# A wait ahead of the sampled tokens' memory-key products and other pauses in a hybrid decoder step

## The chip, the cores and the metric

The kernel runs on one core of one Trainium2 chip, in one launch. The metric is the device time of that launch in microseconds (us). Three runs of the kernel before took 2145.94, 2152.03 and 2154.46 us, so the median is 2152.03 us.

## What is computed

One step of a one-layer hybrid decoder, for a prompt of 1024 tokens and for 8 sampled tokens of other sequences. A norm and one wide projection feed four head groups (differential attention A, RWKV-7 B, Mamba-2 C, cross-attention X into 256 memory tokens); each group's output is gated, the four are concatenated, and a second projection and a last norm follow. What the change touches is X for the samples and the output of C. Cut to these, and with what they read:

```python
h = rmsnorm(x, lp['norm_g'])
p = h @ lp['w_in']
dq, dk, dvv, dg, rs, rg, mz, mxbc, mdt, xq, xg = split_in(p)
...
ym, ssm_new = ssd_scan(xh * dt[..., None], A * dt, bh, chh, ssm_state.astype(f32), chunk)
ym = ym + lp['d_skip'][:, None] * xh
out_m = rmsnorm(ym.reshape(b, t, BRANCH) * jax.nn.silu(mz.astype(f32)), lp['gnorm_g'])
...
qx = xq.reshape(b, t, H_X, D_X)
s = jnp.einsum('bqhd,bmhd->bhqm', qx, mem_k.astype(qx.dtype), preferred_element_type=f32) * (D_X ** -0.5)
pm = jax.nn.softmax(s, axis=-1)
ox = jnp.einsum('bhqm,bmhd->bqhd', pm, mem_v.astype(f32))
out_x = ox.reshape(b, t, BRANCH) * jax.nn.silu(xg.astype(f32))

mixed = jnp.concatenate([out_a, out_b, out_m, out_x], axis=-1).astype(xdtype)
x = x + mixed @ lp['w_out']
```

## The kernel before

**The stream of projections.** The 1024 prompt tokens and 8 sample tokens are three groups of 344 columns. A block of 128 output columns of `w_in` or `w_out` is 16 tiles of the contraction times three groups, and each product is three matmuls, since every float is split into a high and a low part (`hh`, `hl` of the activations, `whi`, `wlo` of the weights). A block is cut into four pieces of four contraction tiles; a piece's weights come by one DMA of 256 KB on SyncE's queue (`raw`, L525) and are split by ScalarE (`whi`, L541) and VectorE (`wlo`, L542). These matmuls (`acc`, L565) are the bulk of TensorE's work; a narrow block for the Mamba step sizes is L583. A finished group is evacuated by ScalarE and VectorE (`evs` L678 to L687 for the RWKV columns, `evg` and `evo` L751 to L754 for the gates).

**The lanes.** The four head groups are written as Python generators, the lanes. A driver hands out instructions while the program is built. It keeps a clock of its own, `K.now`, that only TensorE instructions advance; a lane that says `yield 2.5` is asked again when that clock is 2.5 further, and in between the driver issues matmuls of the projection stream. `yield from K.wait("x")` holds a lane until another lane has said `K.mark("x")`. So a pause sets how many `acc` matmuls stand on TensorE between two steps of a lane. Under this sits the framework's scheduler, which gives each engine its final order; a VectorE instruction needs not stand there in the order in which the lanes issued it.

**Stages.** Lanes run in stages, each with its own memory pools: first A for the prompt; then `lane_x` (cross-attention of the prompt, 4 heads of 4 query blocks) beside `lane_sa` (A and then X for the samples); then RWKV in three lanes, `products`, `elements` and `norm`, beside `lane_b` (the samples' RWKV); then the step sizes, and Mamba's eight chunks in `mixer_m` beside `samples_m`; then the output projection. A stage begins when every lane of the one before has ended.

**Around the change.** `samples_x` runs 22 turns over 16 tiles of the memory keys (`sxkp`, 128 x 512, loaded by GpSimd's queue, 8 buffers). From the seventh turn on a tile is multiplied by its query, spread over the partitions (`sxqb`, loaded on SyncE's queue), and summed by head into `sxsc`; these are two VectorE instructions each, L1766 and L1767. Then come transposes of the scores (`p_sxs`), a softmax, transposes of the weights (`p_sxw`), and 11 turns over the memory values (`sxvp`, products `p_sxo`, columns picked by `p_vc` into `sxo`). On the same VectorE the prompt's `lane_x` takes maxima (`xm` L1715), and divides by the row sums (`xe` L1721) ahead of TensorE's transposes `p_xt`.

After that stage the RWKV stage loads its constants (`cst` L842, `up` L845), a strip of decay inputs (`lw` L864, a tanh on ScalarE, L865) and the first rows (`rkv` L870), and its first matmuls are `p_lora` from `lw` and `up`, then transposes `p_kn` of `kk` and `p_kb` of `rx`.

In `mixer_m`, a chunk's output `my` is multiplied by its gate (L1341, from the transposes `p_mg`), squared and summed (L1344), scaled (L1347) and transposed (`p_my`). A pause of 3.6 stands ahead of `p_my`.

Of the kernel before, what the change touches and what calls it, by code (L numbers as in the profile page):

```python
# [1255 lines left out]
def mixer_m(K, P, dt):  # L1256
# [15 lines left out]
    for c in range(8):  # L1272
        t0 = c * 128
        r8 = nxt
        x = P.tile([128, 4, 128], F32, name="mxx", tag="mxx")
# [69 lines left out]
        nc.vector.tensor_scalar(ss[:, 0:1], ss[:, 0:1], 0.25 / 512, RMS_EPS, op0=ALU.mult, op1=ALU.add)  # L1345
        K.powm(ss[:, 1:2], ss[:, 0:1], 1)
        nc.vector.tensor_scalar(flat(y), flat(y), ss[:, 1:2], 0.5, op0=ALU.mult, op1=ALU.mult)  # L1347
        yield 3.6
        p = K.ps("p_my", 1)
        for b in range(4):  # L1350
            K.tp(p[:, b * 128:b * 128 + 128], flat(y[:, 2 * b:2 * b + 2, :]), K.id)
# [221 lines left out]
def value_columns(K, P, po, o, half, ring, **slot):  # L1573

    nc = K.nc
    e = P.tile([128, 512], F32, name="vce", **slot)
    nc.scalar.copy(e, po)
    yield 1.0
    p = K.ps("p_vc", ring)
    for b in range(4):  # L1580
        K.tp(p[:, b * 128:b * 128 + 128], e[:, b * 128:b * 128 + 128], K.id)
    nc.vector.tensor_copy(out=o.rearrange("p (h b) -> p b h", h=4)[:, 4 * half:4 * half + 4, :],
                          in_=p.rearrange("p (b h r) -> p b h r", b=4, h=4)[:, :, :, 0])
# [156 lines left out]
def samples_x(K, P):  # L1740
    nc, I = K.nc, K.I
    x = P.tile([128, 8, 4], F32, name="sxx", tag="sxx")
# [11 lines left out]
    for i in range(16 + 6):  # L1754
        if i < 16:
            if i % 2 == 0:
                qb = P.tile([128, 512], F32, name="sxqb", tag="sxqb", bufs=4)
                nc.sync.dma_start(out=qb, in_=K.svX[i // 2 * 4:i // 2 * 4 + 4].rearrange(
                    "(o h) c -> o (h c)", o=1).to_broadcast([128, 512]))
            kp = P.tile([128, 512], F32, name="sxkp", tag="sxkp", bufs=8)  # L1760
            nc.gpsimd.dma_start(out=kp, in_=I["cache_mem_k"][i // 2, i % 2 * 128:i % 2 * 128 + 128])
            ahead.append((kp, qb))
        if i >= 6:
            b, a = (i - 6) // 2, (i - 6) % 2
            kp, q = ahead.pop(0)
            nc.vector.tensor_tensor(kp, kp, q, op=ALU.mult)  # L1766
            nc.vector.tensor_reduce(sc[:, a, b * 4:b * 4 + 4], kp.rearrange("p (h c) -> p h c", h=4), axis=AX.X, op=ALU.add)  # L1767
        yield 2.5 if i >= 6 else 1.2
    yield 8.92
    p = K.ps("p_sxs", 0)  # L1770
    for a in range(2):
# [16 lines left out]
    for b in range(8 + 3):  # L1788
        if b < 8:
            vp = [P.tile([128, 512], F32, name="sxvp", tag="sxkp", bufs=8) for a in range(2)]  # L1790
            for a in range(2):
                nc.gpsimd.dma_start(out=vp[a], in_=I["cache_mem_v"][b, a * 128:a * 128 + 128])
            ahead.append(vp)
        yield 4.0 if b > 2 else 1.5
        if b < 3:
            continue
        vp, b = ahead.pop(0), b - 3
        if b % 4 == 0:
            po = K.ps("p_sxo", 0)
        for a in range(2):  # L1800
            for h in range(4):
                q = slice(32 * h, 32 * h + 32)
                K.mm(po[q, (b % 4) * 128:(b % 4) * 128 + 128], lhsT=w[:, a, b * 4 + h:b * 4 + h + 1].to_broadcast([128, 32]),
                     rhs=vp[a][:, h * 128:h * 128 + 128], start=a == 0, stop=a == 1)
        if b % 4 == 3:
            yield from value_columns(K, P, po, o, b // 4, 0, tag="vce")
# [234 lines left out]
def lane_m(K):  # L2041
    yield from K.wait("mz3", 0.00)
    with K.tc.tile_pool(name="mmp", bufs=1, side="right") as P:
        yield from mixer_m(K, P, K.dt)
    K.mark("m")


def lane_sa(K):

    pool = lambda n: K.tc.tile_pool(name=n, bufs=1, side="right")  # L2050
    with pool("sap") as P:
        yield from samples_a(K, P)
    K.mark("sa")
    with pool("sxp") as P:
        yield from samples_x(K, P)
    K.mark("sx")
# [84 lines left out]
```

## Time and profile before

| | |
|---|---|
| median of three runs | 2152.03 us |
| the profiled execution, its own time | 2149.52 us |
| its span from the first to the last instruction | 2147.8 us |
| TensorE, matmuls | 2086.2 us busy, 97% of the span |
| TensorE, weight loads | 1979.4 us busy, 92% |
| VectorE | 1145.8 us, 53% |
| ScalarE | 839.1 us, 39% |
| mean granted TensorE clock | 0.993 of full speed |

TensorE's matmuls and weight loads overlap each other. The span less the matmuls' busy time, 61.6 us, is what TensorE spent without a matmul. The other engines' shares say little by themselves: they count only where TensorE waits for one of them.

### The profile page before, as it was taken

The numbers are of one execution on the slowest core, as the hardware profiler recorded it, in microseconds if no ns is written. First come the engines' busy times: TensorE is split into PE (matmuls) and PEld (weight loads), VectorE is DVE, ScalarE is ACT, GpSimd is POOL, SyncE is SP. The second block draws the span as 40 slices with busy tenths as digits, with TensorE's granted clock in tenths as the row PEclk, the third lists the DMA queues.
The fourth block names the chain that finished last, engine by engine and source line by source line (L and its number), as shares of the span: only waits on it lengthen the run. The fifth ranks groups of instructions, "written<-read, shape, count | busy, mean of one in ns | idle before, by whom it ended". The sixth has DMA issues, their size and how long they took to land.

```text
span 2147.8 us, 41628 instructions
## 1 busy us (share of the span) xinstructions
PE 2086.2 (97%) x16260; PEld 1979.4 (92%) x16260; DVE 1145.8 (53%) x2795; ACT 839.1 (39%) x2231; POOL 203.4 (9%) x286
## 2 busy tenths in 40 slices
PE   8999999999999999999999999999999999999997
PEld 6799999999999989988888888889999999999997
DVE  5724353533643352158877776755966354333554
ACT  6724354443113322145455444432122144333544
POOL 2100000000622210011110010001100000000000
PEclk9999999999999999999999999999999999999998
DMA  7643425242844462332222222226644583222881
GB/s 256 194 131 92 133 76 151 70 128 59 244 144 140 143 217 67 105 74 74 71 69 60 53 61 65 58 67 156 184 137 133 169 253 102 73 73 70 245 247 53
DMA packets 336925, 263.12 MB, mean 123 GB/s; under 512 B 62204, under 2 KB 310986, under 8 KB 336032
## 3 DMA queue, kind: packets, MB, share of 16 engines
q1 hardware_dynamic: 323744, 218.64, 36.3%
q0 software_dynamic: 12320, 40.28, 6.2%
q8 instruction: 128, 2.10, 0.4%
q10 hardware_dynamic: 664, 1.54, 0.2%
q14 instruction: 69, 0.57, 0.1%
HBM read 205.65 MB, written 54.80 MB: 121 GB/s over the span
## 4 chain that ended last, share of the span: by engine, by line
PE 79%; DVE 7%; DMA 5%; issue 4%; ACT 4%; POOL 2%; SPq 0%; ACTq 0%; DVEq 0%; POOLq 0%
PE acc L565 62%; PE p_s L1507 2%; PE p_t L186 2%; PE p_o L186 2%; DMA raw<-in_w_in 1%; DVE wlo L542 1%; DVE evc L716 1%; PE p_wt L190 1%; PE p_out L190 1%; PE acc L583 1%; PE p_xo L186 1%; POOL gst L216 1%; PE p_xs L186 1%; PE p_yd L186 1%; DMA xt<-in_x_prompt 1%
## 5 line engine op out<-in xcount | busy, mean ns | idle before, releaser
L565 PE MATMUL acc<-hh,whi 128*128 128x344 f32 x3312 | 1074.4, 324 | 8.9 <-DVE evg L752 2.9
L565 PE MATMUL acc<-hl,whi 128*128 128x344 f32 x3312 | 1077.2, 325 | 0.0
L565 PE MATMUL acc<-hh,wlo 128*128 128x344 f32 x3312 | 1075.6, 325 | 1.2 <-DVE wlo L542 0.8
L565 PEld LDWEIGHTS acc<-hh,whi 128*128 128x128 f32 x3312 | 624.5, 189 | 15.9 <-DVE evg L752 4.1
L565 PEld LDWEIGHTS acc<-hl,whi 128*128 128x128 f32 x3312 | 625.7, 189 | 5.1 <-issue 0.6
L565 PEld LDWEIGHTS acc<-hh,wlo 128*128 128x128 f32 x3312 | 622.9, 188 | 8.0 <-DVE wlo L542 3.1
L542 DVE TENSOR_TENSOR wlo<-raw,whi 128x512 fp32r<-128x512 f32 x300 | 207.1, 690 | 463.8 <-ACT whi L541 462.4
L541 ACT CAST whi<-raw 128x512 fp32r<-128x512 f32 x300 | 185.5, 618 | 443.9 <-PE acc L565 407.5
L186 PEld LDWEIGHTS p_t<-rt,lt 64*64 64x64 f32 x1280 | 44.6, 134 | 33.6 <-issue 13.3
L1832 ACT ACTIVATE p_out<-xo 128x128 f32<-128x128 f32 (+1 forms) x144 | 39.9, 277 | 77.4 <-DVE xo L1831 73.1
L186 PE MATMUL p_t<-rt,lt 64*64 64x64 f32 (+1 forms) x1280 | 54.3, 223 | 15.8 <-DVE lt L973 7.3
L1510 DVE CUSTOM_DVE_ANT_0 ae<-p_s,al 128x512 f32<-128x512 f32 (+3 forms) x96 | 49.6, 554 | 34.9 <-PE p_s L1507 34.9
L1517 ACT ACTIVATE ae<-ae,am 128x128 f32<-128x128 f32 (+7 forms) x64 | 49.2, 772 | 10.9 <-DVE am L1514 10.8
L1831 DVE TENSOR_TENSOR xo<-xo,p_out 128x128 f32<-128x128 f32 (+1 forms) x144 | 39.4, 280 | 26.0 <-PE p_out L190 25.7
L979 ACT COPY rt<-p_t 128x256 f32<-128x256 f32 x64 | 22.0, 344 | 77.3 <-DVE xc L971 72.7
L542 DVE TENSOR_TENSOR wlo<-oraw,whi 128x512 fp32r<-128x512 f32 x48 | 33.2, 692 | 31.7 <-ACT whi L541 31.4
L216 POOL TENSOR_TENSOR osr<-osr,mhalf 128x1 f32<-128x1 f32 (+1 forms) x9 | 6.4, 725 | 461.4 <-DMA xo<-in_x_prompt 337.6
L216 POOL TENSOR_TENSOR ass<-ass,mhalf 128x8 f32<-128x8 f32 x4 | 6.6, 1642 | 423.3 <-DVE ass L1558 423.3
L1507 PE MATMUL p_s<-akm,aqt 128*128 128x512 f32 (+3 forms) x192 | 45.1, 360 | 0.0
L1618 POOL DMA_INDIRECT sakp<-in_cache_diff_k,sapt x32 | 42.0, 1313 | 31.2 <-DMA xmk<-smk 18.1
L541 ACT CAST whi<-oraw 128x512 fp32r<-128x512 f32 x48 | 29.7, 618 | 32.5 <-PE acc L565 31.1
L1834 DVE TENSOR_TENSOR xo<-xo,fgc 128x128 f32<-128x128 f32 (+1 forms) x96 | 27.0, 288 | 28.7 <-ACT p_out L1832 27.6
(467 smaller groups left out, 2587.0 us busy)
## 6 DMA issues: line engine op xcount, KB each, us to landing
raw<-in_w_in SPq DMA_DIRECT2D x220, 256.0 KB
raw<-in_w_out SPq DMA_DIRECT2D x80, 256.0 KB
oraw<-in_w_out SPq DMA_DIRECT2D x12, 1024.0 KB
evm<-sm SPq DMA_DIRECT2D x48, 172.0 KB
sB<-evs SPq DMA_DIRECT2D x39, 172.0 KB
sA<-evp SPq DMA_DIRECT2D x36, 172.0 KB
evo<-so SPq DMA_DIRECT2D x36, 172.0 KB
sm<-evo SPq DMA_DIRECT2D x36, 172.0 KB
```

Source lines behind the costliest of these rows:

```text
L186: self.nc.tensor.matmul(out, lhsT=lhsT, rhs=rhs, start=start, stop=stop, **k)
L190: self.nc.tensor.transpose(out, in_, ident)
L216: self.nc.gpsimd.tensor_tensor(out, x, self.mhalf[:P, :n], op=ALU.pow)
L541: nc.scalar.copy(hi, raw)
L542: nc.vector.tensor_tensor(lo, raw, hi.bitcast(F32), op=ALU.subtract)
L565: nc.tensor.matmul(acc[g][:, :G], lhsT=x[:, k, :], rhs=y, start=kp == ko[0] and k == 0 and x is hi and y is a, stop=kp == ko[-1] and k == ...
L1507: nc.tensor.matmul(p[:, :k1 - k0], lhsT=qt[:, a, c], rhs=km[:, c, k0:k1], start=a == 0, stop=a == 1)
L1510: nc.vector.tensor_tensor_reduce(e[:, c, k0:k1], p[:, :k1 - k0], al[:, x0:x0 + k1 - k0], 1.0, -3e38, ALU.add, ALU.max, m[:, c, pc:pc + 1])
L1517: nc.scalar.activation(e[:, c, :nk], e[:, c, :nk], AF.Exp, bias=m[:, c, 0:1], accum_out=z[:, c:c + 1])
L1618: nc.gpsimd.indirect_dma_start(out=dst, out_offset=None, in_=I[src].rearrange("a p c -> (a p) c"), in_offset=bass.IndirectOffsetOnAxis(ap= ...
L1831: nc.vector.tensor_tensor(xt, xt, q[:n, k * 128:k * 128 + 128], op=ALU.add)
L1832: nc.scalar.activation(q[:n, k * 128:k * 128 + 128], xt, AF.Square, accum_out=self.ss[:n, 3 * g + k, cb:cb + 1])
```

## The change

Three pauses and one wait are changed. `samples_x` waits for the end of the prompt's cross-attention before it issues the first product of a memory key; its turns from there on pause 1.8 where they paused 2.5; the turns over the memory values pause 3.0 where they paused 4.0. In the first of Mamba's eight chunks the pause ahead of `p_my` is 5.0 where it was 3.6. No instruction is added or taken away.

```diff
@@ -1345,7 +1345,7 @@
-        yield 3.6
+        yield 3.6 if c else 5.0
         p = K.ps("p_my", 1)
@@ -1760,12 +1760,14 @@
             ahead.append((kp, qb))
+        if i == 6:
+            yield from K.wait("x")
         if i >= 6:
             b, a = (i - 6) // 2, (i - 6) % 2
             kp, q = ahead.pop(0)
             nc.vector.tensor_tensor(kp, kp, q, op=ALU.mult)
             nc.vector.tensor_reduce(sc[:, a, b * 4:b * 4 + 4], kp.rearrange("p (h c) -> p h c", h=4), axis=AX.X, op=ALU.add)
-        yield 2.5 if i >= 6 else 1.2
+        yield 1.8 if i >= 6 else 1.2
     yield 8.92
@@ -1791,7 +1793,7 @@
-        yield 4.0 if b > 2 else 1.5
+        yield 3.0 if b > 2 else 1.5
```

How the built program's order changes is shown at three places. The lines of `samples_x` stand two further down in the changed file, so L1766 and L1767 there are L1768 and L1769.

First VectorE, where the products of the memory keys (`sxkp`, `sxsc`) begin, among the prompt's maxima and divisions (`xm`, `xe`) and a split of weights (`wlo`). Before:

```order
L1766 TENSOR_TENSOR sxkp<-sxkp,sxqb 128x512 x2
L1767 TENSOR_REDUCE sxsc<-sxkp 128x4
L542 TENSOR_TENSOR wlo<-raw,whi 128x512
L1767 TENSOR_REDUCE sxsc<-sxkp 128x4
L1715 TENSOR_REDUCE xm<-p_xs 128x2
L1766 TENSOR_TENSOR sxkp<-sxkp,sxqb 128x512
L1716 TENSOR_SCALAR xm<-xm 128x2
L1766 TENSOR_TENSOR sxkp<-sxkp,sxqb 128x512
L1767 TENSOR_REDUCE sxsc<-sxkp 128x4
L1720 RECIPROCAL xm<-xm 128x2
L1767 TENSOR_REDUCE sxsc<-sxkp 128x4
L1721 TENSOR_TENSOR xe<-xe,xm 128x512
```

With the change:

```order
L1768 TENSOR_TENSOR sxkp<-sxkp,sxqb 128x512 x2
L1769 TENSOR_REDUCE sxsc<-sxkp 128x4
L542 TENSOR_TENSOR wlo<-raw,whi 128x512
L1769 TENSOR_REDUCE sxsc<-sxkp 128x4
L1715 TENSOR_REDUCE xm<-p_xs 128x2
L1768 TENSOR_TENSOR sxkp<-sxkp,sxqb 128x512
L1716 TENSOR_SCALAR xm<-xm 128x2
L1768 TENSOR_TENSOR sxkp<-sxkp,sxqb 128x512
L1769 TENSOR_REDUCE sxsc<-sxkp 128x4
L1720 RECIPROCAL xm<-xm 128x2
L1769 TENSOR_REDUCE sxsc<-sxkp 128x4
L1721 TENSOR_TENSOR xe<-xe,xm 128x512
```

Nothing moved here: row for row it is the same order, and it stays the same on VectorE until the maximum over the scores `p_sxs`. On TensorE the first row that differs is the pair of transposes `p_sxs` itself, which stand behind 184 more `acc` matmuls than before (3960 against 3776, counted from the program's start).

Second SyncE's queue, where the last of the samples' cross-attention (`so<-sxo`) is followed by the first loads of the RWKV stage. Before:

```order
L525 DMA raw<-in_w_in 128x4x8 x2
L1807 DMA so<-sxo 128x4x8
L842 DMA cst_9313<-in_cst 128x992
L525 DMA raw<-in_w_in 128x4x8
L845 DMA up<-in_up 128x512
L864 DMA lw<-sB 128x256
L870 DMA rkv<-sB 128x4x64
L687 DMA sB<-evs 128x344
L870 DMA rkv<-sB 128x4x64
```

With the change:

```order
L525 DMA raw<-in_w_in 128x4x128 x2
L1809 DMA so<-sxo 128x4x8
L842 DMA cst_9479<-in_cst 128x992
L525 DMA raw<-in_w_in 128x4x128
L845 DMA up<-in_up 128x512
L864 DMA lw<-sB 128x256
L870 DMA rkv<-sB 128x4x64
L525 DMA raw<-in_w_in 128x4x128
L870 DMA rkv<-sB 128x4x64 x2
```

The queue's own order is nearly the same, but the place moved against TensorE: between the last `p_vc` and the first `p_lora` there stand 48 `acc` matmuls, where 120 stood; from the first `p_lora` to the first `p_z` there are 148, where 172 stood. From the program's start the first `p_lora` stands behind 48 more `acc` matmuls, and the end of the RWKV lanes behind 24 more.

Third VectorE in the first Mamba chunk, where `my` is gated (L1341) and scaled (L1347); L1282 is the scan over the next chunk's decays, `evg` and `evo` are the evacuation of a gate block. Before:

```order
L1335 TENSOR_TENSOR St<-St,p_st 128x512
L1282 SCALAR_TENSOR_TENSOR r_17170<-r_17170,lt 128x1024
L1341 TENSOR_TENSOR my<-my,p_mg 128x512
L542 TENSOR_TENSOR wlo<-raw,whi 128x512
L1345 TENSOR_SCALAR myss<-myss 128x1
L1347 TENSOR_SCALAR my<-my,myss 128x512
L752 SCALAR_TENSOR_TENSOR evg<-evg,acc_17021 128x344
```

With the change:

```order
L1335 TENSOR_TENSOR St<-St,p_st 128x512
L1282 SCALAR_TENSOR_TENSOR r_17194<-r_17194,lt 128x1024
L752 SCALAR_TENSOR_TENSOR evg<-evg,acc_17021 128x344
L753 SCALAR_TENSOR_TENSOR evo<-evg,evo 128x344
L1341 TENSOR_TENSOR my<-my,p_mg 128x512
L752 SCALAR_TENSOR_TENSOR evg<-evg,acc_17022 128x344
L753 SCALAR_TENSOR_TENSOR evo<-evg,evo 128x344
L1345 TENSOR_SCALAR myss<-myss 128x1
L1347 TENSOR_SCALAR my<-my,myss 128x512
```

Four evacuating instructions now stand ahead of the scaled `my`, where one split of weights stood. On TensorE 36 `acc` matmuls stand between the transposes `p_mg` and `p_my` of this chunk, where 28 stood.

## Rows read from the trace of the kernel before

**Rows 1.** The page's first part: span, busy time of each engine.

```profile
span 2147.8 us, 41628 instructions
PE 2086.2 (97%) x16260; PEld 1979.4 (92%) x16260; DVE 1145.8 (53%) x2795; ACT 839.1 (39%) x2231; POOL 203.4 (9%) x286
```

**Rows 2.** Busy time by stretch: start:end, length, engines, clock, DMA share, GB/s.

```profile
906.00:935.00 29.00, 29.00 (x197) 24.38 (x195) 7.61 (x24) 12.12 (x33) 2.72 (x6) 1.00 0.37 95
935.00:1445.00 510.00, 492.00 (x5804) 440.83 (x5803) 380.78 (x1009) 235.35 (x708) 55.04 (x102) 1.00 0.25 64
1490.00:1500.00 10.00, 7.38 (x50) 7.06 (x49) 5.22 (x8) 3.03 (x7) 0.57 (x1) 1.00 0.39 116
1500.00:1690.00 190.00, 189.04 (x1251) 185.43 (x1251) 128.09 (x195) 38.95 (x76) 10.04 (x16) 1.00 0.51 144
771.30:778.00 6.70, 5.42 (x18) 5.09 (x19) 5.91 (x10) 1.09 (x3) 2.25 (x5) 0.51 0.88 264
...
1054.60:1058.00 3.40, 3.40 (x16) 3.34 (x15) 3.40 (x10) 3.04 (x10) 1.42 (x4) 0.52 0.66 188
```

**Rows 3.** Waits of TensorE, 680 to 800: in total, times, longest (us).

```profile
PE p_xt L190 <- DVE xe L1721: 4.1, 2, 3.6
```

**Rows 4.** VectorE in order of time, 738 to 792: start, us, instruction, idle before.

```profile
760.05 1.30 DVE L1766 TENSOR_TENSOR sxkp<-sxkp,sxqb 128x512 f32<-128x512 f32 x2 [8.07 <-DMA sxqb<-svX]
```

**Rows 5.** TensorE in order of time, 765 to 782.

```profile
768.47 0.32 PE L565 MATMUL acc<-hl,whi 128*128 128x344 f32 x1
768.63 0.32 PE L565 MATMUL acc<-hh,wlo 128*128 128x344 f32 x1
772.58 1.09 PE L190 MATMUL p_xt<-cst,xe 128*128 128x128 f32 x4 [3.63 <-DVE xe L1721]
```

**Rows 6.** DMA issues: line engine, count, KB each, us to landing.

```profile
sxvp<-in_cache_mem_v POOLq DMA_DIRECT2D x16, 256.0 KB, 3.5
```

**Rows 7.** The start of the RWKV stage, 900 to 945, TensorE in order of time.

```profile
905.62 0.60 PE L190 MATMUL p_vc<-cst,vce 128*128 128x128 f32 x4
...
926.44 1.57 PE L186 MATMUL p_lora<-lw,up 64*128 64x128 f32 x16
...
931.11 0.38 PE L190 MATMUL p_kn<-cst,kk 128*128 128x128 f32 x2
```

**Rows 8.** The same stretch on SyncE's queue, then ScalarE, then VectorE.

```profile
906.47 0.37 SPq L1807 DMA_DIRECT2D so<-sxo  x1
...
910.82 0.42 SPq L864 DMA_DIRECT2D lw<-sB  x1
...
914.20 0.42 ACT L865 ACTIVATE lw<-lw 64x256 f32<-64x256 f32 x1 [0.45 <-DMA lw<-sB]
...
916.46 0.42 DVE L786 TENSOR_TENSOR kk<-rkv,pt 128x256 f32<-128x256 f32 x1
...
934.93 0.29 DVE L800 COPY rx<-rn 128x256 f32<-128x256 f32 x1 [0.95 <-POOL rn L216]
```

**Rows 9.** TensorE right behind: the transposes that need `rx`.

```profile
935.28 0.44 PE L190 MATMUL p_kb<-cst,rx 128*128 128x128 f32 x2
```

**Rows 10.** Waits of TensorE, 906 to 1445: the first of ten rows.

```profile
PE p_t L186 <- DVE lt L973: 7.3, 9, 2.3
```

**Rows 11.** VectorE in the first Mamba chunk, in order of time, 1490 to 1505.

```profile
1493.69 2.29 DVE L1282 TENSOR_TENSOR_SCAN r<-r,lt 128x1024 f32<-128x1024 f32 x1 [2.90 <-DMA r<-sda]
1495.90 0.66 DVE L1341 TENSOR_TENSOR my<-my,p_mg 128x512 f32<-128x512 f32 x1
...
1499.22 0.49 DVE L1347 TENSOR_SCALAR my<-my,myss 128x512 f32<-128x512 f32 x1 [0.69 <-POOL myss L216]
1499.62 0.51 DVE L752 SCALAR_TENSOR_TENSOR evg<-evg,acc 128x344 f32<-128x344 f32 x1
```

**Rows 12.** TensorE there: the transposes that need `my`.

```profile
1499.85 0.63 PE L190 MATMUL p_my<-cst,my 128*128 128x128 f32 x4 [2.62 <-DVE my L1347]
```

**Rows 13.** ScalarE there: the squares of `my`, in order of time.

```profile
1497.63 0.63 ACT L1344 ACTIVATE mysq<-my 128x512 f32<-128x512 f32 x1
```

## The prediction, made before the changed kernel ran

> **What bounds the kernel now.** I read the page's first part, then the table of stretches, then TensorE's waits in the stretches that the change touches, and last the order of time around each wait. The first part shows TensorE with a matmul in flight for 2086.2 of 2147.8 us [rows 1]: the time of this kernel is TensorE's work plus 61.6 us of holes. The change adds and removes no instruction, so it can only fill or open holes, or change the clock in which matmuls run. The reader is to look for three things in the table of stretches [rows 2]: how much of each stretch is without a matmul, whether the granted clock is 1.00, and which stretch comes behind a step that moves. In the stage of the cross-attentions the holes are two, both for `xe` and 4.1 us together [rows 3]; the first 29 us of the RWKV stage have none; the remaining 510 us of that stage have 18.0; around the first chunk's `p_my` 2.6 of 10 us are lost; the rest of the Mamba stage loses 1.0 in 190 [rows 2].
>
> Where the larger hole for `xe` comes from is told by the order of time. VectorE came to the first two products of memory keys and stood 8.07 us for `sxqb` [rows 4]; the maxima and divisions of the prompt's attention stood behind them, and TensorE, whose matmuls start 0.16 us apart at full clock, stood 3.63 us for `xe` at 772.58 [rows 5]. Then the clock fell: from 771.3 to 778.0 the granted clock was 0.51, that is 1.2 in place of 2.4 GHz [rows 2].
>
> **The change, part by part.**
>
> *The wait for the prompt's attention, and the pause of 1.8.* The words of the change would take that hole away: 4.1 us of waits, and the slow clock behind them. Of the slow stretch, 772.58 to 778.0 had matmuls, 5.4 us at half speed, so 2.7 us lost; 6.8 us in all. The page "TensorE: Matmul & The Clock Gate" of the Trainium skill (Terms) puts the penalty at the throttled time multiplied by one minus the granted share; its estimate here is 6.7 x 0.5 = 3.4 us and 7.5 in all, as it also counts the 1.3 us in which TensorE had nothing to run. But the built order, shown above, says that nothing of this happens. On VectorE the products stand exactly where they stood, the wait for `sxqb` is still ahead of the same `xe`, and no row of TensorE differs before `p_sxs`. A pause of a lane spaces TensorE's steps; the scheduler below puts a VectorE product where VectorE is free, and the two instructions in question have no TensorE step ahead of them in their lane. I take 0 for this part; the ends are 0 and a gain of 6.8.
>
> *The tail of the samples' cross-attention, later by 184 matmuls.* `p_sxs` and all behind it move down TensorE's stream by some 29 us. What hides it is the stream itself: between two turns of memory values there are 24 `acc` matmuls in place of 32, 3.8 us in place of 5.1. A tile of values is loaded four turns ahead, at least 15 us, and lands in 3.5 [rows 6]. Nobody but the gates of X waits for the result, and they come hundreds of us later. 0 us; if the cover were gone, a late tile would stop TensorE for what is left of those 3.5 us.
>
> *The start of the RWKV stage, which is now close behind.* This is where something new can wait. Before, 120 `acc` matmuls lay between the last `p_vc` and `p_lora`; now 48. So 72 x 0.16 = 11.5 us of cover go. Before, the tanh of `lw` ended at 914.62 and `p_lora` began at 926.44 [rows 7, 8]: 11.8 us of slack, of which 0.3 is left. The chain ahead of it is the same: `so<-sxo`, then the load of constants, a weight load, `up`, `lw`; 8.4 us from the end of `p_vc` (906.22) to the end of the tanh [rows 7, 8], on a queue on which a weight load that waits for VectorE holds up those behind it. `kk` ended at 916.88 and `p_kn` began at 931.11 [rows 7, 8]: 14.2 us, and 76 matmuls fewer (the 72, and 16 in place of 20 behind `p_lora`) take 12.2, so 2.0 are left; its second load of rows now stands behind a weight load. `rx` ended at 935.22 and `p_kb` began at 935.28 [rows 8, 9], no slack at all, and there are 14 matmuls in place of 24 between `p_kn` and `p_kb`: up to 1.6 us of wait, less what ScalarE and VectorE save because the evacuation of the narrow block (`evd`) is now over by then. Up to `p_z` the first unit has 24 matmuls fewer, so it can lose 3.8 us at most as long as its loads are in time. Ends 0 and 3.8; I take 1.0, nearer the low end, because only the last of the three steps has no slack.
>
> *The other units of the RWKV stage.* All of it stands 24 to 48 matmuls later against the lanes, so its meetings with the evacuation of projection blocks are dealt anew. Its 18.0 us of holes [rows 2] are mostly `p_t` waiting for `lt`, 7.3 us in 9 times [rows 10]. In the order I counted, over the 64 rounds, the VectorE instructions that stand between a round's transpose and its mask `lt`: 36 before, 40 now. In proportion, 7.3 x 4 / 36 = +0.8 us. The page "Perfetto Trace Analysis" (Optimization Strategy) says that the same gap repeating on the engine that should be saturated can mean too few buffers; if so the order would not matter, and this term would be 0 and the sum 0.8 lower. The rows name VectorE's `lt`, not a buffer, as what ended these waits, so I keep +0.8. For the ends I take half of the 18.0 us either way, +9 and -9.
>
> *The pause of 5.0 in the first Mamba chunk.* `p_my` waited 2.62 us for `my` [rows 12]. Eight matmuls more ahead of it are 1.3 us of cover. Against that, two evacuating instructions, 0.51 us each [rows 11], now stand ahead of the gated `my`. But ScalarE began its squares at 1497.63 [rows 13], 1.07 us after the gated `my` was there at 1496.56 [rows 11], being busy with other work; so nearly all of that 1.0 us is free. The second pair falls beside the squares. I take 0.3 us of delay and a gain of 1.0; ends 0 and 1.3. A part of the wait stays in any case. No clock to win: it was 1.00 through that hole [rows 2]. In the other seven chunks the lanes of prompt and samples stand 1.4 apart from where they stood; with 1.0 us of holes in 190 [rows 2] I take 0, ends -1 and +1.
>
> **The sum:** 0 + 0 + 1.0 + 0.8 - 1.0 + 0 = +0.8 us. Against the profiled execution's own 2149.52 that is 2150.3. That execution lies 2.5 us under the median of the three runs, 2152.03; for the median I forecast 2152.8. About 0.5%, 10.8 us, is what a measurement of this kernel can tell from no change.
>
> **The rivals.**
>
> 1. *A late load stops the RWKV stage, and the change is slower.* The place is the first `p_lora`, the price is that of the hole for `xe`. For it: of 11.8 us of slack 0.3 is left, and the chain of five DMAs stands on a queue that weight loads can hold up. Against it: a delay of 1 or 2 us costs just that, and the hole of 2.62 us left the clock at 1.00; behind the one of 3.63 it fell, and once in the RWKV stage, for 3.4 us behind the longest hole there, of 2.3 [rows 2, 5, 10, 12]. So it decides when the tanh of `lw` ends over 10.5 us behind `p_vc`, 2 us and more later than the 8.4 of before. Then 3.6 + 2.7 for clock, and 3.8 in `p_kn` to `p_z` in place of 1.0: +9.1 more, 2161.9, and with a bad deal of the units beyond 2163. By the clock page's estimate of 3.4 in place of 2.7 it would be 2162.6. Chance 0.10.
> 2. *The units of the RWKV stage fall well.* Half of the holes or more are gone: 2152.8 - 9.8 = 2143, more in the best case. For it: nothing but chance decides which evacuation stands ahead of which `lt`. Against it: the count of 40 against 36. Chance 0.09.
> 3. *The products do move.* Then 6.8 us go: 2146.0. For it only the words of the change; against it the order, row for row. Chance 0.03.
>
> The forecast, little change because the named move does not take place, has 0.78.
>
> **How the numbers follow.** The forecast's own spread, from the ends of the terms, is 2144 to 2161. The range reaches down into the second rival and up to the first: 2143 to 2162. Faster by over 0.5% needs under 2141.3: the better part of the second rival, 0.06. Slower by over 0.5% needs over 2162.8: half of the first rival and a bad deal without it, 0.09. Within 0.5%: 0.85.
>
> **What the new profile would show.** Right: the hole for `xe` of about 3.6 us and the clock at half behind it, at the same place and unchanged; `p_sxs` some 29 us later; `p_lora` less than 10 us behind the last `p_vc`, with holes of 2 us at most there and at `p_kn` and `p_kb`; the hole at the first `p_my` smaller by about 1 us, not gone. Wrong: no wait for `xe` between 765 and 780, which would make the third rival true; a hole over 3 us at `p_lora` with a granted clock of 0.5 behind it, the first; holes of the RWKV stage far from 18 us, the second or its opposite.

## The result and the profile after

Four runs of the changed kernel took 2171.93 to 2173.36 us, median 2172.12; the kernel before, on the same chip, 2150.03 (four runs). The ratio is 1.0096, with a 95% interval of 1.0071 to 1.0121: slower by 22 us. The forecast was 2152.8 and the range ended at 2162, so it was wrong, and on the side to which it gave 0.09.

The page's first part of the kernel after, to be read against [rows 1]:

```profile
span 2170.4 us, 41611 instructions
PE 2098.4 (97%) x16260; PEld 1987.4 (92%) x16260; DVE 1144.9 (53%) x2795; ACT 841.6 (39%) x2231; POOL 202.0 (9%) x286
```

The same 16260 matmuls, 22.6 us more of span. Of these 10.4 are TensorE without a matmul (72.0 us where it was 61.6), and 12.2 are matmuls that took longer. The table of stretches of the kernel after (columns as in [rows 2]) shows a part of both:

```profile
774.60:778.00 3.40, 2.30 (x9) 2.33 (x10) 3.40 (x7) 0.62 (x2) 1.07 (x2) 0.57 0.95 283
935.00:1455.70 520.70, 502.77 (x5843) 447.69 (x5843) 383.01 (x1017) 241.18 (x721) 56.85 (x103) 1.00 0.25 64
1502.83:1509.60 6.77, 6.77 (x28) 6.47 (x29) 2.71 (x5) 0.00 (x0) 0.00 (x0) 0.55 0.39 128
...
1596.80:1600.20 3.40, 3.37 (x16) 3.40 (x17) 0.69 (x1) 0.00 (x0) 0.00 (x0) 0.63 0.50 142
1753.30:1756.70 3.40, 3.38 (x16) 3.38 (x16) 0.77 (x2) 0.62 (x1) 0.00 (x0) 0.70 0.58 154
```

To find the place, both traces are cut at the same instructions of TensorE. Between two cuts the built order gives the number of `acc` matmuls; where it differs, 0.158 us is allowed for each, their median spacing. What is left over is the loss of the stretch:

| stretch | `acc` before, after | us before, after | loss, us |
|---|---|---|---|
| start to the last `p_xo` | 3640, 3640 | 822.5, 824.1 | +1.7 |
| to the first `p_lora` | 600, 648 | 104.0, 110.8 | -0.8 |
| to the last `p_so` (RWKV) | 1900, 1876 | 518.1, 520.7 | +6.4 |
| to the first `p_dt` | 97, 97 | 15.7, 15.7 | 0 |
| to the first `p_yd` | 135, 135 | 24.6, 31.4 | +6.9 |
| to the first `p_my` | 52, 60 | 15.0, 16.5 | +0.2 |
| to `p_sst` (the other chunks) | 892, 892 | 182.6, 187.5 | +4.9 |
| to the last matmul (the output) | 2716, 2684 | 450.8, 448.7 | +3.0 |

The first line is not the change's: up to there the order is the same. Nothing was lost where the edits of `samples_x` stand. All of it came later.

**The start of Mamba.** TensorE in order of time, after:

```profile
1502.83 3.65 PE L186 MATMUL p_yd<-xdt,r 128*128 128x64 f32 x16 [5.41 <-ACT whi L541]
...
1519.29 0.60 PE L190 MATMUL p_my<-cst,my 128*128 128x128 f32 x4
```

`p_yd` waited 5.41 us where it had not waited at all, and behind it the clock was 0.55 for 6.8 us (table of stretches, third row), 3.0 us lost. The releaser named here is ScalarE's `whi`, but ScalarE itself had just stood 7.9 us for VectorE's `r` (L1293). VectorE in order of time shows who was late:

```profile
1500.13 0.20 DVE L1381 COPY smv<-smx 128x32 f32<-128x32 f32 x1 [7.74 <-DMA smx<-sM]
1500.23 0.17 DVE L1382 COPY smv<-smx 128x32 f32<-128x32 f32 x1
1500.31 1.22 DVE L1293 TENSOR_TENSOR r<-r,gm 128x1024 f32<-128x1024 f32 x1
...
1502.05 0.68 DVE L1303 TENSOR_TENSOR xdt<-p_x,dt 128x512 f32<-128x512 f32 x1
```

VectorE stood 7.74 us for `smx`, 32 KB of the samples' Mamba inputs, with the two operands of `p_yd` (`r`, `xdt`) queued behind the copy; `xdt` was ready at 1502.73, 0.1 us ahead of `p_yd`. SyncE's queue of the kernel after, and GpSimd's:

```profile
1485.48 0.31 SPq L1265 DMA_DIRECT2D r<-sda  x1
1486.26 0.38 SPq L525 DMA_DIRECT2D raw<-in_w_in  x1
1486.75 0.45 SPq L1380 DMA_DIRECT2D smx<-sM  x1
```
```profile
1486.21 4.16 POOL L1417 DMA_DIRECT2D sms<-in_state_ssm  x8 [14.07 <-ACT sme L1392]
```

The same two queues before, and VectorE's copy:

```profile
1474.14 0.32 SPq L1265 DMA_DIRECT2D r<-sda  x1
1474.56 0.38 SPq L1380 DMA_DIRECT2D smx<-sM  x1
```
```profile
1474.87 4.16 POOL L1417 DMA_DIRECT2D sms<-in_state_ssm  x8 [13.66 <-ACT sme L1392]
```
```profile
1480.64 0.18 DVE L1381 COPY smv<-smx 128x32 f32<-128x32 f32 x1
```

Before, `smx` left 0.31 us ahead of GpSimd's eight state loads of 256 KB and was there 6.1 us later, without a wait. After, a weight load had come between `r` and `smx`, so `smx` left 0.54 us behind the first state load and landed after 13.4.

**The other chunks and the output.** Waits of TensorE from 1510 to 1800 (in total, times, longest), before and then after:

```profile
PE acc L565 <- DVE evg L752: 2.9, 4, 1.0
PE p_my L190 <- DVE my L1347: 0.3, 1, 0.3
```
```profile
PE p_my L190 <- DVE my L1347: 4.0, 4, 2.4
PE acc L565 <- DVE evg L752: 3.5, 1, 3.5
```

After the change the longest of each (at 1596.8 and 1753.3) has a stretch of low clock behind it (above). The second came from a load, too; VectorE, after:

```profile
1752.33 0.52 DVE L753 SCALAR_TENSOR_TENSOR evo<-evg,evo 128x344 f32<-128x344 f32 x1 [5.04 <-DMA evo<-so]
```

**The RWKV stage.** Here the waits did not grow. The row of `lt` L953 before, which stands beside [rows 10], and then the first rows of TensorE's waits after:

```profile
PE p_t L186 <- DVE lt L953: 2.8, 7, 0.8
```
```profile
PE p_t L186 <- DVE lt L973: 5.6, 9, 1.6
PE p_t L186 <- DVE lt L953: 4.1, 8, 0.9
PE p_t L186 <- DVE gst L1086: 3.0, 2, 1.9
```

All holes of the stage make 17.9 us, before 18.0. The loss is in the matmuls' spacing. Summed over successive matmuls, waits left out: from lane to lane 149.0 us (before 144.6, with 3777 and 3780 pairs), between a lane and `acc` either way 69.6 (65.6; 376 changes, 360), from `acc` to `acc` 284.2 (289.9), of which the 24 `acc` matmuls fewer explain 3.8.

### The profile page after: what moved, and what is told of

It is laid out like the page before. It is cut to its first block, busy times and chain, and to the rows that moved or that the text cites. A ratio compares the mean times of both kernels' runs of the same rounds, so it can differ in the third digit from the quotient of the medians.

```text
span 2170.4 us, 41611 instructions
## 1 busy us (share of the span) xinstructions
PE 2098.4 (97%) x16260; PEld 1987.4 (92%) x16260; DVE 1144.9 (53%) x2795; ACT 841.6 (39%) x2231; POOL 202.0 (9%) x286
## 5 line engine op out<-in xcount | busy, mean ns | idle before, releaser
L565 PEld LDWEIGHTS acc<-hh,whi 128*128 128x128 f32 x3312 | 626.0, 189 | 22.6 <-ACT rawB L686 5.0
L542 DVE TENSOR_TENSOR wlo<-oraw,whi 128x512 fp32r<-128x512 f32 x48 | 33.2, 692 | 31.4 <-ACT whi L541 31.2
L716 DVE SCALAR_TENSOR_TENSOR evc<-evx,der,evc 128x344 f32<-128x344 f32 (+1 forms) x72 | 40.2, 565 | 3.6 <-ACT evc L714 3.3
```

The lines of the kernel that those rows point to most:

```text
L542: nc.vector.tensor_tensor(lo, raw, hi.bitcast(F32), op=ALU.subtract)
L565: nc.tensor.matmul(acc[g][:, :G], lhsT=x[:, k, :], rhs=y, start=kp == ko[0] and k == 0 and x is hi and y is a, stop=kp == ko[-1] and k == ...
L716: nc.vector.scalar_tensor_tensor(e[:, :n], x[:, t:t + n], w(t), e[:, :n], op0=ALU.mult, op1=ALU.add)
```

## The experiments

The table gives each kernel's losses against the trace of before, one profile each, worked out as above. The ratios in the text are times over that of the kernel before, with their 95% intervals. In the RWKV column the stretches of low clock are taken out (every 4 us below 0.97, at the time times one minus the clock, against 1.6 us before), because they come and go between executions. Medians are to be compared with before on the same chip only: 2150.7 for e1 to e4, 2154.8 for e5 to e8, 2150.8 for e9 to e12, 2155.9 for e13 to e15. Columns: `acc` matmuls ahead of the first `p_my`; then the losses.

| kernel | median us | `acc` | RWKV | `p_dt` to `p_yd` | to `p_my` | chunks | output |
|---|---|---|---|---|---|---|---|
| after | 2172.1 | 6456 | 6.3 | 6.9 | 0.2 | 4.9 | 3.0 |
| e1_x_only | 2165.0 | 6448 | 5.7 | 8.0 | 0.4 | 1.1 | -0.6 |
| e2_pause_only | 2150.9 | 6432 | -0.5 | 0.3 | -1.7 | 4.1 | -1.4 |
| e3_smx_early | 2158.9 | 6456 | 6.7 | 1.0 | -2.8 | 3.3 | 3.6 |
| e4_smx_late | 2148.7 | 6424 | 0.0 | 1.4 | -0.7 | 0.4 | -1.3 |
| e5_shift_back | 2155.3 | 6432 | 0.6 | 0.3 | -1.1 | 3.8 | -1.5 |
| e6_shift24 | 2170.2 | 6448 | 5.2 | 7.0 | 0.5 | 0.7 | 0.6 |
| e7_shift32 | 2174.4 | 6456 | 7.6 | 0.8 | -1.4 | 5.2 | 4.2 |
| e8_half_burst | 2154.8 | 6424 | -0.6 | 1.1 | -1.1 | 1.0 | -1.1 |
| e9_sms_held | 2169.1 | 6456 | 6.1 | 1.1 | 4.3 | 5.0 | 3.9 |
| e10_svx_early | 2148.3 | 6424 | -0.3 | 1.4 | 0.8 | 0.5 | -0.7 |
| e11_groups194 | 2168.9 | 6432 | 6.3 | 8.7 | 0.0 | 2.0 | -1.5 |
| e12_groups176 | 2181.3 | 6544 | 4.7 | 10.3 | -2.8 | 0.9 | 11.1 |
| e13_loads_early | 2152.7 | 6424 | -0.9 | 0.5 | 2.9 | 2.2 | -2.1 |
| e14_offset_back | 2165.2 | 6484 | 1.4 | 0.1 | 1.7 | -1.3 | 10.5 |
| e15_lead_lost | 2153.4 | 6424 | 2.0 | 0.1 | 0.1 | 2.5 | -1.9 |

e11, e12, e14 and e15 were run once.

### The two halves of the change

e1_x_only is the changed kernel without the pause of 5.0, e2_pause_only the kernel before with it:

```diff
-        yield 3.6
+        yield 3.6 if c else 5.0
```

> Only the edits of samples_x (the wait, the pauses of 1.8 and 3.0); the first Mamba chunk keeps its pause of 3.6. Theory: the extra time comes from the shift of everything behind the samples' cross-attention, above all from a load of the samples' Mamba inputs (smx) that now leaves behind a weight load and behind the eight state loads of 256 KB. Then p_yd of the first chunk waits about 5 us again, the clock falls to half behind it, and the time is 2166 to 2174. Rival: the longer pause in the first chunk costs the time, for instance through the order of VectorE behind it. Then this kernel is at 2150 to 2155 and p_yd does not wait.

> Only the pause of 5.0 in the first Mamba chunk. Theory: 2147 to 2153, within 0.3% of before, with the wait for the first p_my smaller than 2.6 us and no wait of p_yd over 1 us. Rival (the pause costs the time): 2160 or more.

e1 measured 1.0064 (1.0040 to 1.0087), e2 1.0004 (0.9992 to 1.0015). The edits of `samples_x` are enough for the hole; in e1 it was 6.79 us long. The pause alone costs nothing that can be measured: the stretch with the first `p_my` gained 1.7 us, and the other chunks lost 4.1. Added to the edits of `samples_x` it put the chunks 8 `acc` matmuls later (6448 to 6456), and the chunks and the output lost 7 us more in the traces. The intervals of e1 and of the changed kernel overlap, so by times alone that is not shown.

### Nothing but a shift, back and forth

e5_shift_back keeps the wait, the 1.8 and the 5.0, but ends early:

```diff
-        yield 3.0 if b > 2 else 1.5
+        yield 2.2 if b > 2 else 1.5
```

e6_shift24 and e7_shift32 are the kernel before with one pause ahead of the samples' end:

```diff
         yield from samples_x(K, P)
+    yield 16.4
     K.mark("sx")
```

(17.2 in e7.)

> The changed kernel, but with the turns over the memory values at a pause of 2.2 in place of 3.0, so that the samples' cross-attention ends early enough for the RWKV stage to start where it started before (first p_lora behind 4240 acc matmuls again); the wait, the pause of 1.8 and the pause of 5.0 stay. Theory (only the shift of the later stages costs time): RWKV stage 518 to 520 us, no hole over 1.5 us at the first p_yd, 2148 to 2154. Rival (the wait or the pauses cost time where they stand): 2160 or more.

> The kernel before, with nothing but a pause of 16.4 behind the samples' cross-attention: the RWKV stage ends 24 acc matmuls later, as in the changed kernel, and in the built order the load of smx stands behind a weight load again. Theory: the RWKV stage takes 4 to 9 us more than its matmuls account for, p_yd of the first chunk waits 4 to 7 us, and the time is 2161 to 2168. Rival: without the wait and the pauses of the change the shift alone is harmless, 2148 to 2153.

> As the last, with a pause of 17.2: 8 acc matmuls further, where the built order has the load of smx directly behind that of r again. Theory: the RWKV stage loses 3 to 9 us as in the last, but p_yd waits less than 2 us, so 2153 to 2159, some 7 to 9 us under the last kernel. Rival (the place of the smx load is not what decides, only how far the stage is shifted): the same time as the last kernel, within 2 us.

e5 measured 1.0008 (0.9984 to 1.0031), with the RWKV stage and the start of Mamba as before. e6 measured 1.0067 (1.0043 to 1.0092), with `p_yd` waiting 3.86 us and the RWKV loss back. So what the change says it does costs nothing that can be measured; that it ends late does. e7 measured 1.0077 (1.0044 to 1.0110). Its `smx` left directly behind `r`, 0.17 us behind the first state load, and `p_yd` did not wait, as expected. The time was not 7 to 9 us under that of e6, though. Part of this lies ahead of the shift (in this execution the stretch to the last `p_xo` alone was 11.5 us longer than in the trace of before, in that of e6 3.7); but e7 also stands at 6456, and the four kernels at 6456 lost 3.3 to 5.2 in the chunks and 3.0 to 4.2 in the output, the two at 6448 at most 1.1 and 0.6. In the waits of TensorE from 1510 to 1800 of e1 the same two rows read:

```profile
PE acc L565 <- DVE evg L752: 2.1, 3, 0.8
PE p_my L190 <- DVE my L1347: 1.6, 3, 0.7
```

About as many waits, but short ones, none over 0.8 us, and the granted clock was not low again between 1512 and 1800.

### The load behind the burst

e3_smx_early is the changed kernel with the load of `smx` asked for in the step-size stage; e4_smx_late is the kernel before with `smx` behind `sdM`; e9_sms_held is the changed kernel with the state tiles in the memory of `smx`, so that GpSimd can't begin before the copy. The edits of e3 and then of e9, cut:

```diff
+    K.smx = PD.tile([128, 8, 8], F32, name="smx", tag="smx")
+    nc.sync.dma_start(out=K.smx, in_=K.sM[:, :, T:TT].rearrange("b p t -> p b t"))
     yield 6.80
     p = K.ps("p_ex", 1)
...
-    xs = P.tile([128, 8, 8], F32, name="smx", tag="smx")
-    nc.sync.dma_start(out=xs, in_=K.sM[:, :, T:TT].rearrange("b p t -> p b t"))
+    xs = K.smx
```

```diff
-    xs = P.tile([128, 8, 8], F32, name="smx", tag="smx")
+    xs = P.tile([128, 4, 8, 128], F32, name="smx", tag="sms").rearrange(
+        "p k a b -> p (k a b)")[:, :64].rearrange("p (a b) -> p a b", b=8)
...
-    ss = []
+    S4 = P.tile([128, 4, 8, 128], F32, name="sms", tag="sms")
+    ss = [S4[:, k] for k in range(4)]
     for k in range(4):
-        ss.append(P.tile([128, 8, 128], F32, name="sms", tag="sms", bufs=4))
```

> The changed kernel, but with the load of smx issued in the step-size stage, ahead of sda and of the state loads. Theory: VectorE no longer stands 7.7 us for smx, the hole of 5.4 us at the first p_yd falls below 2 us, and the clock is not halved behind it (6.8 us of half clock were 3.4 us lost): 6 to 9 us less than the changed kernel, 2163 to 2166; what is left above before, 13 to 16 us, comes from the other places. Rival: the load of r (512 KB, also late by 3.4 us) or the state loads themselves hold the chunk; then the hole stays above 4 us and the time within 2 us of 2172.

> The kernel before, with the load of smx put behind that of sdM on SyncE's queue, so that it leaves after the state loads have begun, as in the changed kernel; nothing else is moved. Theory: the load lands 8 us later or more, VectorE stands for it, p_yd waits 3 to 6 us and the clock falls behind it: 6 to 10 us slower than before, 2156 to 2160. Rival: the load's place does not matter, the time is within 2 us of before.

> The changed kernel, with the eight state loads on GpSimd's queue held back until VectorE has copied smx (the state tiles take over the memory in which smx lies); the order on TensorE and VectorE is that of the changed kernel, row for row, and on SyncE's queue smx still stands behind the weight load. Theory: the 2 MB of state loads are what smx waits for; without them it lands in 6 us or less, the hole at the first p_yd falls from 5.4 to under 2 us, and the time is 7 to 10 us under the changed kernel, 2161 to 2165. Rival: the weight load ahead of smx on the same queue delays it; then smx still takes over 10 us, the hole stays over 4 us, and the time within 2 us of the changed kernel.

e3 measured 1.0045 (1.0028 to 1.0063), an interval that does not touch that of the changed kernel; 11 us came back by the ratios, 13 by the medians, more than was expected. Its TensorE in order of time:

```profile
1492.65 1.89 PE L186 MATMUL p_yd<-xdt,r 128*128 128x64 f32 x16
...
1506.17 0.60 PE L190 MATMUL p_my<-cst,my 128*128 128x128 f32 x4
```

No wait, and 1.89 us for the sixteen matmuls of `p_yd`, not 3.65 as at the low clock. By the table, `p_dt` to `p_my` lost 8.9 us less than in the changed kernel; the rest is in the start, ahead of the change (4.7 us between these two executions), and in the chunks.

e4 missed: 0.9995 (0.9981 to 1.0009). `smx` left 0.11 us behind the first state load and took 9.0 us, VectorE stood 2.87 for it, but `p_yd` only 1.11. So being behind the start of the burst is not enough; in e7 the load took 8.7. In the five kernels that lost over 5 us here `smx` left later still, 0.5 to 2.1 us behind the first state load, and took 13.4 (after), 14.8 (e1), 12.2 (e6), 14.2 (e11) and 14.0 us (e12). In four of them a weight load of 256 KB stood between `r` and `smx` and went first: in e6 it left 2.0 us behind `r`, and `smx` only then. In e12 none did, only a load of 172 KB for the gates (`evo`). What waited there was not `p_yd` but `p_bt`, an earlier step of the chunk. VectorE and TensorE, e12:

```profile
1519.28 0.20 DVE L1381 COPY smv<-smx 128x32 f32<-128x32 f32 x1 [4.61 <-DMA smx<-sM]
...
1519.46 0.42 DVE L1290 TENSOR_TENSOR gm<-p_g,cst 128x256 f32<-128x256 f32 x1
```
```profile
1519.93 0.69 PE L190 MATMUL p_bt<-cst,mxb 128*128 128x128 f32 x2 [8.83 <-DVE gm L1290]
```

e9 takes away the state loads and leaves the weight load where it was. VectorE, e9:

```profile
1492.10 0.19 DVE L1381 COPY smv<-smx 128x32 f32<-128x32 f32 x1
```

`smx`, issued at 1486.50, was there within 5.6 us, without a wait, and `p_yd` had none. So the delay needs the state loads. Whether the load ahead on SyncE's own queue adds to it, or only sends `smx` off later into the burst, no run separates; in e7 a weight load left 1.03 us ahead of `smx`, in front of `r`, and `smx` took 8.7 all the same. The page "DMA: Bandwidth & Descriptors" of the Trainium skill (Issuing engines are not separate DMA queues) says that DMAs of any engine run on the same 16 DMA engines and interleave; by that rule GpSimd's loads can hold up `smx` on SyncE's queue, and these traces agree (at most 5.6 us without them, 8.7 to 14.8 where it left behind the first).

The time did not fall, though a fall had been expected: it was 1.0089 (1.0054 to 1.0123). The state loads now met the next load of `r`. VectorE, and TensorE behind it, in e9:

```profile
1508.58 2.29 DVE L1282 TENSOR_TENSOR_SCAN r<-r,lt 128x1024 f32<-128x1024 f32 x1 [5.58 <-DMA r<-sda]
1510.79 0.49 DVE L752 SCALAR_TENSOR_TENSOR evg<-evg,acc 128x344 f32<-128x344 f32 x1
```
```profile
1511.33 0.66 PE L565 MATMUL acc<-hh,whi 128*128 128x344 f32 x1 [4.41 <-DVE evg L752]
```

The hole moved from `p_yd` to `acc`. Here holding the burst back only chose another victim; moving the small load ahead of it had none at this place.

### Why the RWKV stage is dearer

e11_groups194 and e12_groups176 are e6 with pauses of 14 and 30. e14_offset_back is the changed kernel with a pause ahead of the RWKV lanes; e15_lead_lost is the kernel before with a later `lane_b`.

```diff
         yield from K.wait(f"rs{RS[-1]}", 6.0)
+        yield 4.0
```

```diff
-    yield from K.wait(f"rs{RS[-1]}", 2.0)
+    yield from K.wait(f"rs{RS[-1]}", 6.0)
```

> The kernel before with a pause of 14 behind the samples' cross-attention: the RWKV stage ends only 8 acc matmuls later, but its stream changes between the projection's matmuls and a lane's 14 times more often (194 stretches of acc in place of 180; the changed kernel has 188). Theory (the 6.4 us more of the RWKV stage are the price of these changes, not of waits): 11 us more than before from p_lora to p_so after allowing 0.157 us for each acc matmul, 7 to 14. Rival (the distance of the shift, or chance waits, decide): under 5.

> The same with a pause of 30: the RWKV stage ends 120 acc matmuls later, with 176 stretches of acc, 4 fewer than before. Theory (changes between the two kinds of matmul cost the time): -3 to +2 us in the RWKV stage after allowing for the acc matmuls. Rival (any shift away from the old place costs it some 6 us): 5 or more.

> The changed kernel, with a pause of 4.0 ahead of the RWKV lanes, behind their wait. Before, the samples' RWKV (lane_b, which waits for the last RWKV block and 2.0) started 4.0 ahead of them (they wait 6.0); in the changed kernel, as in every kernel with a late end of the cross-attention, both waits are over and all start together. Theory (this lost lead is what makes the RWKV stage dearer): p_lora to p_so is within 2.5 us of before after allowing 0.157 us for each acc matmul and taking out the low clock. Rival (the lead does not matter; the later place against the projection's pieces does): 4.5 to 7.5 us more, as in all shifted kernels.

> The kernel before, with nothing but lane_b waiting 6.0 in place of 2.0 behind the last RWKV block, so that it starts together with the RWKV lanes; the RWKV stage begins and ends where it did, and all behind it stands as before. Theory (the lost lead): the RWKV stage takes 4 to 7 us more than before after allowing for the acc matmuls and the low clock. Rival: within 2 us of before.

e11, with 194 stretches of `acc` where the changed kernel has 188, lost 8 us as it stands, inside the theory's 7 to 14, but 6.3 with the low clock taken out, no more than the changed kernel. e12 brought the theory of changes between `acc` and lanes down, with fewer stretches than before (176) and still 4.7 us lost. e14 gave the samples' lane its lead of 4.0 back: 1.4 us are left of 6.3, and lane to lane takes 147.1 us, not 149.0. But e15, which takes only the lead away, lost 2.0, not 4 to 7. So neither the lost lead (2.0) nor a shift with the lead kept (1.4) makes the 6.3 us of both. The lanes of e14 also end 28 `acc` matmuls later than those of the changed kernel, so its 1.4 belongs to another place. By kinds of neighbours the 4.4 us from lane to lane are spread: the most in the changed kernel is 1.2 us for `p_s` behind `p_v` (five times, never before) and 1.0 from `p_lora` to `p_lora`. Why these stand apart stays open; no hole shows it. e14 then lost 10.5 in the output, with waits for `evg` of 6.3 us in all: the next place against the blocks, the next losses.

### Towards a kernel faster than both

If bursts hold up small loads, the 8 us for `sxqb` [rows 4] might be the same. e8_half_burst halves the burst of memory keys:

```diff
-            kp = P.tile([128, 512], F32, name="sxkp", tag="sxkp", bufs=8)
+            kp = P.tile([128, 512], F32, name="sxkp", tag="sxkp", bufs=4)
...
-            vp = [P.tile([128, 512], F32, name="sxvp", tag="sxkp", bufs=8) for a in range(2)]
+            vp = [P.tile([128, 512], F32, name="sxvp", tag=("sxkp", "sxqb")[a], bufs=4) for a in range(2)]
```

> The kernel before, with four buffers in place of eight for the first memory keys, so that GpSimd's queue begins with four tiles of 256 KB instead of eight; the second tiles of the memory values share buffers with sxqb. The order on TensorE and VectorE is the same row for row. Theory (what holds up smx in Mamba is what holds up sxqb here: a load on SyncE's queue that leaves behind a burst of GpSimd's): VectorE stands 3 to 5 us for sxqb in place of 8.07, the hole of 3.6 us for xe falls below 1 us and the clock stays at full, 2143 to 2147. Rival: the 8 us are the chain of the store of svX and the load of sxqb themselves; then the hole stays at 3 us or more and the time within 1 us of before.

It missed, at 1.0000 (0.9981 to 1.0019). VectorE, e8:

```profile
759.50 1.29 DVE L1766 TENSOR_TENSOR sxkp<-sxkp,sxqb 128x512 f32<-128x512 f32 x2 [7.26 <-DMA sxqb<-svX]
```

7.26 in place of 8.07: the chain itself is long (the store of `svX` at 750.95, the first `sxqb` at 755.73). So e10_svx_early begins the chain earlier, inside `samples_a` (the edit is cut):

```diff
+        if b == 6:
+            px = K.ps("p_sxx", 0)
+            K.tp(px[:32, :128], sx.rearrange("p s h -> p (s h)"), K.id)
...
+            nc.sync.dma_start(out=K.svX, in_=rows)
         yield 6.5 if b else 2.0
...
```

> The kernel before, with the sampled tokens' queries (sxq, p_sxx, svX) turned and stored some 20 us earlier, inside the last turns of the samples' attention A, so that sxqb can be loaded as soon as its buffers are there. Theory: VectorE no longer stands 8 us for sxqb, no hole over 1 us for xe, no half clock at 770 to 780: 4 to 7 us less than before, 2144 to 2147 on a chip on which before takes 2150. Rival: VectorE then stands as long for the memory keys or for sxqb behind the eight key loads; hole of 3 us or more, time within 1 us of before.

TensorE in order of time and the table of stretches, e10:

```profile
766.64 0.60 PE L190 MATMUL p_xt<-cst,xe 128*128 128x128 f32 x4
...
769.57 0.63 PE L190 MATMUL p_xt<-cst,xe 128*128 128x128 f32 x4 [1.07 <-DVE xe L1732]
```
```profile
766.00:776.00 10.00, 8.93 (x59) 8.54 (x58) 10.00 (x20) 3.63 (x9) 3.76 (x7) 1.00 0.86 275
```

The hole of 3.63 is gone, the clock is 1.00, and the last `p_xo` came 5.7 us earlier than in the trace of before. In time it is 0.9987 (0.9968 to 1.0006), 2.5 us between medians: not told apart from no change, as the stretch ahead of it scatters by as much. e13_loads_early adds the early `smx` and a second buffer for `r`, and asks for the next chunk's `r` at a chunk's start (cut to the buffer):

```diff
-        r8 = P.tile([128, 8, 128], F32, name="r8", tag="r8")
+        r8 = P.tile([128, 8, 128], F32, name="r8", tag="r8", bufs=2)
```

> The kernel before, with three loads moved ahead: svX stored during the samples' attention A (as in the earlier run), smx loaded in the step-size stage, and a second buffer for Mamba's rows r, so that the next chunk's 512 KB are asked for at a chunk's start. Theory: the hole for xe stays at about 1 us at full clock; the scan over r no longer stands late ahead of the gated my, so the first p_my waits under 1.5 us in place of 2.6 to 3.4; 5 to 9 us less than before. Rival: the second load of r now meets the eight state loads earlier and the first r lands late, with a hole at p_g, p_bt or p_yd of the first chunk of 2 us or more; then no gain over the run with svX alone.

e13 measured 0.9992 (0.9972 to 1.0012). The first `p_my` waited 5.57 us, not under 1.5. The second chunk's `r` came in time, but the scan over the third chunk's now stands where that over the second's stood, ahead of the gated `my`; VectorE, e13:

```profile
1489.66 2.29 DVE L1285 TENSOR_TENSOR_SCAN r<-r,lt 128x1024 f32<-128x1024 f32 x1 [5.85 <-DMA r<-sda]
1491.87 0.66 DVE L1343 TENSOR_TENSOR my<-my,p_mg 128x512 f32<-128x512 f32 x1
```

So the second buffer only put the next chunk's load in the same place. No kernel of the study is shown to be faster than the one before.

## Why the prediction was wrong

**The products do not move: right.** The hole for `xe` is where the forecast left it; VectorE and TensorE in order of time, after:

```profile
763.17 1.29 DVE L1768 TENSOR_TENSOR sxkp<-sxkp,sxqb 128x512 f32<-128x512 f32 x2 [7.96 <-DMA sxqb<-svX]
```
```profile
775.70 1.09 PE L190 MATMUL p_xt<-cst,xe 128*128 128x128 f32 x4 [3.63 <-DVE xe L1721]
```

7.96 us against 8.07 [rows 4], 3.63 against 3.63 [rows 5], and a clock of 0.57 behind it (first row of the stretches). That the order decides, not the words of the change, held. What the words do bring if the chain is really moved, e10 shows: 5.7 us in that stretch.

**The tail of the samples' cross-attention: right**, 0 us; `p_xo` to `p_lora` lost nothing.

**The start of the RWKV stage: right.** TensorE in order of time, after, against [rows 7, 9]:

```profile
926.00 0.60 PE L190 MATMUL p_vc<-cst,vce 128*128 128x128 f32 x4
...
934.95 1.16 PE L186 MATMUL p_lora<-lw,up 64*128 64x128 f32 x16
...
939.39 0.44 PE L190 MATMUL p_kn<-cst,kk 128*128 128x128 f32 x2
943.06 0.41 PE L190 MATMUL p_kb<-cst,rx 128*128 128x128 f32 x2 [1.02 <-DVE rx L800]
```

Less than 10 us behind `p_vc`, no wait at `p_lora` or `p_kn`, 1.02 at `p_kb`: the forecast's 1.0. The first rival, a late load at `p_lora`, did not come; its mechanism did, 570 us further on.

**The other units of the RWKV stage: the term was mis-sized, and taken from the wrong quantity.** It was +0.8, from the count of VectorE instructions ahead of `lt`. The waits for `lt` did not grow (7.3 and 2.8 before, 5.6 and 4.1 after), and the loss of 6.4 lies between the holes. Its ends of 9 either way did hold it. Of the rule that repeated gaps can mean too few buffers (the page "Perfetto Trace Analysis" of the Trainium skill, Optimization Strategy) the prediction said that by it the order would not matter; the holes agree with that, 18.0 and 17.9, but no run here changed those buffers.

**The pause of 5.0, and "in the other seven chunks ... I take 0, ends -1 and +1": this is the step that failed.** For the first `p_my` the forecast was a gain of 1.0 with a part of the wait left; the wait went altogether, 2.62 us [rows 12]. But the prediction followed the shift of 24 `acc` matmuls only to the end of the RWKV lanes. It read the Mamba stage as it stood, with 1.0 us of holes in 190 [rows 2], and took that calm for a property of the stage. It was one of the place: 24 matmuls further the start of the stage loses 6.9 us and 3.0 more to the clock (less the 2.6 won at the first `p_my`); with the 8 of the longer pause, 32 further, the chunks lose 4.9 and the output 3.0. Of the sum, +0.8 forecast and some 21 measured without the start, some 15 belong to places for which the prediction had 0 or, for the stage's start and the output, no term at all. Its spread of 2144 to 2161 is narrower than the ends of its terms laid end to end, some 2141 to 2166 without the 6.8; the measured time lies outside both. One sign was there to be read: SyncE's order at the stage's start, where the weight load now stands ahead of `smx`. That `smx` thereby leaves behind the state loads is a matter of time, which the order alone does not give. What makes the chunks and the output lose at their new place was traced only to the waits shown above; no run takes these away.

## What to carry to other kernels

When an edit shifts a stream against the work beside it, compare the order of every DMA queue at the start of every later stage, not only where the edit stands, and ask when each small load leaves against the bursts of the other queues; a small load just ahead of a bulk burst is a place that a shift of 24 matmuls can break. Move such a load well ahead of the burst; holding the burst back only passed the wait on here. And run the shift alone, with none of the edits: here it gave most of the loss (1.0067 and 1.0077 where the change gave 1.0096), and the edits without the shift gave none that could be measured (1.0008).

## What the runs showed of the hardware

A load of 32 KB took at most 5.6 us with no burst beside it (e9) and at most 6.1 where it left 0.3 us ahead of eight loads of 256 KB on another queue (before). It took 8.7 and 9.0 where it left 0.1 to 0.2 us behind the first of them (e7, e4), and 12.2 to 14.8 where it left 0.5 to 2.1 us behind (after, e1, e6, e11, e12). In these five another load, of 256 or 172 KB, also stood right ahead of it on its own queue; its part is not separated. Behind the same eight loads, held back, VectorE stood 5.58 us for a load of `r` (e9).

TensorE's matmuls can lose 4 us in a stage without a hole that a list of waits shows: the lanes' matmuls of the RWKV stage took 144.6 to 144.9 us from one to the next in the seven kernels with the order of before, 147.1 in e14, and 148 to 151 in the eight others that stand later, which have five orders between them (low clock not taken out).
